# One load per projection weight, x brought in transposed, and a sample tile in column quarters, in a convolutional decoder layer on eight cores

## The chip, the cores and the metric

The kernel runs on the eight NeuronCores of one Trainium2 chip, two dies of four cores. Every core executes the same program on its own part of the batch, and no core waits for another. The metric is the device time in microseconds (us) of the slowest core of one execution, taken as the median of several executions. An execution counts as slow when one die is more than 1% longer than the other at a lower granted TensorE clock, or when it is more than 1.5% above the fastest execution of the same kernel; only fast executions are compared below. The granted clock is the share of its full clock that the profile's records show TensorE was given. TensorE writes its results into banks of a buffer called PSUM, which the other engines read and so free again. Loads are issued on two queues, GpSimd's and SyncE's, and both are served by the same 16 transfer (DMA) engines of the core. Engine names in the profile are PE (TensorE), PEld (weight load of TensorE), DVE (VectorE), ACT (ScalarE), POOL (GpSimd) and SP (SyncE, which here only issues transfers).

## The reference

One layer of a trunk, applied to 8 prompt sequences of 2048 tokens (one for each core) and to 128 single sample tokens (16 for each core). The width D is 1024, the hidden width of the two feed-forward networks (FFN) 2816.

```python
def swiglu(x, w_gate, w_up, w_down):
    return (silu(x @ w_gate) * (x @ w_up)) @ w_down

def token_mixers(h, ctx_a, ctx_b, w_in, b_in, w_dw_a, ...):
    z = h @ w_in + b_in                                    # 1024 -> 2560
    a_val, a_gate, g_b, g_c, b_val = split(z, 5 parts of 512)
    u = a_val * sigmoid(a_gate)
    ua, new_ctx_a = causal_depthwise(ctx_a, u, w_dw_a)     # width 31
    ua = silu(layer_norm(ua + b_dw_a, ln_conv_g, ln_conv_b))
    v = g_c * b_val
    vb, new_ctx_b = causal_depthwise(ctx_b, v, w_dw_b)     # width 3
    out = concatenate([ua, g_b * vb]) @ w_o + b_o
    return out, new_ctx_a, new_ctx_b

def trunk_layer(x, ...):
    x = layer_norm(ALPHA * x + 0.5 * swiglu(x, first FFN))
    x = layer_norm(ALPHA * x + token_mixers(x))
    x = layer_norm(ALPHA * x + 0.5 * swiglu(x, second FFN))
    return x, new_a, new_b
```

The outputs are the new x of the prompts and of the samples, and the last 30 and last 2 inputs of the two convolutions.

## The kernel before

A core treats its 2048 + 16 tokens in two blocks (1024 and 1040). `xT` holds x transposed, in bf16, for all tokens; `hT` holds the hidden activations of one block; `RW` is one large buffer that holds the down weights during a down-projection and the mixer's work space between. Every engine executes its list of instructions in the order in which the program emits them, and a small helper, `P.op`, puts a semaphore wait wherever one instruction reads or overwrites what another engine or a transfer has touched. It goes by names such as `("xr", s)`.

An up-projection is a list of groups. One group is 16 matmuls of up to 512 columns (8 for the gate, 8 for the up half), a SiLU pass on ScalarE and a multiplication on VectorE:

```python
def u_group(idx, b, f, g):
    (tok0, n, gi) = g
    l0 = tok0 - b * BLK
    s = idx % NSLOT
    bg, bu, q = ub(), ub(), sgr()

    def mm(e, gu, bk):
        for k in range(KC):
            c = (gu * KC + k) * 128
            ins = e.matmul(bank(bk, n), lhsT=ring[:, s, c:c + 128], rhs=xT[:, k, tok0:tok0 + n],
                           start=(k == 0), stop=(k == KC - 1))
        return ins
    P.op("pe", lambda e: mm(e, 0, bg), reads=[("ring", s, 0)] + xtoks(tok0, n), writes=pst(bg))
    P.op("pe", lambda e: mm(e, 1, bu), reads=[("ring", s, 1)] + xtoks(tok0, n), writes=pst(bu))
    P.op("act", lambda e: e.activation(out=sg[:, q, :n], in_=bank(bg, n), func=AF.Silu),
         reads=pst(bg), writes=[("sg", q)])
    P.op("dve", lambda e: e.tensor_tensor(out=hT[:, f, l0:l0 + n], in0=sg[:, q, :n], in1=bank(bu, n), op=ALU.mult),
         reads=[("sg", q)] + pst(bu), writes=[("hT", f, gi)])

```

`merge` lays other work between the groups. Each item of the second list has a gap: how many up groups follow it. So the mixer of a block is hidden among the matmuls of the next up-projection.

```python
def merge(items, side):
    credit = 0.0
    items = list(items)
    for th, gap in side:
        th()
        credit += gap
        while credit >= 1.0 - 1e-9 and items:
            items.pop(0)()
            credit -= 1.0
    while items:
        items.pop(0)()
```

x is loaded in rows and transposed on TensorE, as is every normed tile that a later matmul reads:

```python
def xpose_from(t, src, rtoks, bk):
    (tok0, n) = tok(t)

    def pe(e):
        for k in range(KC):
            ins = e.transpose(out=psb[:, bk * 1024 + k * n: bk * 1024 + (k + 1) * n],
                              in_=src[:n, k * 128:(k + 1) * 128], identity=ident_bf[:n, :n])
        return ins
    P.op("pe", pe, reads=list(rtoks) + ["ident_bf"], writes=pst(bk))
    P.op("act", lambda e: e.activation(
        out=xT[:, :, tok0:tok0 + n],
        in_=psb[:, bk * 1024: bk * 1024 + KC * n].rearrange("p (k n) -> p k n", k=KC), func=AF.Identity),
        reads=pst(bk), writes=[("xT", t)])
```

The mixer before goes unit by unit, a unit being 512 tokens: for each of four channel chunks five projections (each with its own load of the weight), the convolution input written to DRAM and read back in replicas that are shifted by one token, and 32 matmuls in four column groups. Then follow, per tile of 128 tokens, a norm, SiLU, the output projection (with the bias as a matmul of two rows) and the second norm.

```python
        win_seq = [fo for u in range(4) for ch in range(4) for fo in (4 + ch, ch, 12 + ch, 16 + ch, 8 + ch)]
# ... (in tA)
                P.op("sp", lambda e: e.dma_start(out=uscr[us], in_=U[:, us, :]),
                     reads=[("U", us), ("Uh", us), ("Uz", us)] + MC, writes=[("uscr", us)], dma="us_%d" % us)
# ... (in rep_in)
                for s_ in range(4):
                    P.op("sp", lambda e, s_=s_: e.dma_start(out=R2[32 * s_:32 * s_ + 32, :, :], in_=src[:, :, s_:s_ + R2W]),
                         reads=[("uscr", us)] + MC, writes=[("R2", s_)], dma="r2_%d" % s_)
# ... (in S3)
                    for k in (4, 5, 6, 7, 0, 1, 2, 3):
                        for h in range(2):
                            e.matmul(ps[:n, (4 + h) * 512:(5 + h) * 512], lhsT=lhs(k), rhs=wo[:, k, h * 512:(h + 1) * 512],
                                     start=(k == 4), stop=False)
                    for h in range(2):
                        ins = e.matmul(ps[:n, (4 + h) * 512:(5 + h) * 512], lhsT=ones2[0:2, :n],
                                       rhs=bo2[0:2, h * 512:(h + 1) * 512], start=False, stop=True)
```

The program at its top level, after the first loads. Transposes of x stand between the first up groups, and the lines with `merge` show what is laid beside what:

```python
        for t in range(2):
            x0pose(t)
        u_group(0, 0, 0, (0, 256, 0))
        for t in range(2, 4):
            x0pose(t)
        u_group(0, 0, 0, (256, 256, 0))
        u_group(1, 0, 1, (0, 512, 0))
# ...
        ss = sample_state()
        side = [(lambda: (consts(), ss[0](), load_ln(0)), 2)]
        for i in range(11):
            side.append((lambda i=i: load_wd(0, i), 1.0))
            side.append((ss[1 + i] if i < len(ss) - 1 else (lambda: None), 2.2))
        merge(up_items(0, 0)[4:], side)
# ...
        pend = down(0, 0, 2.0 * ALPHA, 4.0 * EPS, False, aux=aux)
# ...
        merge(up_items(0, 1), side)                     # side: mixer(0, ...)
        load_ln(0)
        pend = down(0, 1, 2.0 * ALPHA, 4.0 * EPS, False, npar=3)
# ...
        merge(up_items(1, 0), side)                     # side: mixer(1, ...)
        load_ln(2)
        down(1, 0, 2.0 * ALPHA, 4.0 * EPS, True, npar=3)
        merge(up_items(1, 1), [])
        down(1, 1, 2.0 * ALPHA, 4.0 * EPS, True)
```

## Time and profile before

Three executions took 1312.84 to 1314.68 us, median 1312.9. A further one was profiled. All cores ran undisturbed: spans of 1295.9 to 1312.2 us, mean granted clock 0.984 to 0.991.

The prediction shows the lines of the page and of the nine stretches. This table is the key to them: idle time of PE in each stretch is its length less the busy time in it.

| Stretch | What runs | PE idle | What PE waits for |
|---|---|---|---|
| (1) | first FFN, up of block 0 | 29.8 | x, its transposes, the convolution state |
| (2) | its down | 1.6 | |
| (3) | up of block 1, mixer of block 0 | 6.5 | replicas of the convolution input |
| (4) | its down | 7.6 | transposes after the norm |
| (5) | second FFN, up of block 0, mixer of block 1 | 13.5 | transposes, replicas, small outputs |
| (6) | its down | 0.6 | |
| (7) | up of block 1 | 2.1 | a product of VectorE |
| (8) | its down | 0 | |
| (9) | after the last matmul | 10.2 | end of the last norm and store |

How to read it: PE is busy for 95% of the time, so what is not taken out of its list must come from the 72 us in which it stands, and some 40% of those are in the first stretch.

### The profile page before, as it was taken

Reading aid. Unit: us, or ns where it says so; the run is one execution under the profiler, and the core shown is the slowest. Engines: PE = TensorE matmul, PEld = TensorE weight load, DVE = VectorE, ACT = ScalarE, POOL = GpSimd, SP = SyncE. Lnnn points to the kernel's source line nnn. Section 1 sums busy time; section 2 is a strip of 40 time slices with the busy share of each in tenths; the row PEclk is TensorE's granted clock in tenths of the full one; section 3 lists DMA queues with packets and bytes.
Section 4 is the critical chain, followed back from the end, with each engine's and each line's share of the span. In section 5 each row is a group of like instructions: output and inputs, shape, how many; then the busy total and the mean of one; then the engine's idle time right before and its main releaser. Section 6 shows DMA issues by size and latency. Waiting matters only on the chain.

```text
span 1312.2 us, 20168 instructions; the slowest of 8 cores (1295.9 to 1312.2 us)
## 1 busy us (share of the span) xinstructions
PE 1240.5 (95%) x7262; PEld 645.5 (49%) x7262; DVE 527.4 (40%) x856; ACT 273.9 (21%) x460; POOL 211.3 (16%) x361
## 2 busy tenths in 40 slices
PE   5599999999999999998989899999999999999996
PEld 4244444445555556553444344445444456666443
DVE  0222124544445544515544345543633632222454
ACT  2111112231123313301121123313420011111000
POOL 2011102211122112111111112102220110000011
PEclk9899999999999999999999999999999999999999
DMA  9686769448865686793237856546777344442122
GB/s 137 132 180 112 123 111 179 135 118 148 168 124 126 136 164 118 159 198 107 67 102 142 163 110 134 123 89 132 148 177 146 128 113 80 69 79 33 51 82 81
DMA packets 65172, 161.54 MB, mean 123 GB/s; under 512 B 6882, under 2 KB 17506, under 8 KB 65059
## 3 DMA queue, kind: packets, MB, share of 16 engines
q0 software_dynamic: 36832, 90.75, 42.8%
q1 hardware_dynamic: 28243, 69.51, 16.6%
q8 instruction: 60, 0.98, 0.3%
q14 instruction: 37, 0.30, 0.1%
...
## 4 chain that ended last, share of the span: by engine, by line
PE 87%; DMA 6%; DVE 2%; issue 2%; ACT 1%; POOL 1%; SPq 0%; POOLq 0%; DVEq 0%; ACTq 0%
PE ps L457 44%; PE ps L521 23%; PE ps L576 10%; PE ps L806 4%; PE ps L694 2%; DMA sb_RW<-wd 2%; PE ps L396 2%; DMA sb_RW<-uscr 1%; DMA sb_hT<-sca 1%; DMA uscr<-sb_RW 1%; DMA sb_ring<-wgu 1%; PE ps L809 1%; PE ps L783 1%; PE ps L758 1%; DVE sb_xr L427 1%
## 5 line engine op out<-in xcount | busy, mean ns | idle before, releaser
L457 PE MATMUL ps<-sb_xT,sb_ring 128*128 128x352 bf16 (+3 forms) x3568 | 639.3, 338 | 13.9 <-ACT sb_xT L400 7.0
L457 PEld LDWEIGHTS ps<-sb_xT,sb_ring 128*128 128x128 bf16 x3568 | 347.9, 99 | 284.8 <-issue 30.6
L521 PE MATMUL ps<-sb_RW,sb_hT 128*128 128x512 bf16 (+1 forms) x1496 | 327.4, 380 | 0.6 <-DMA sb_RW<-wd 0.6
L464 DVE TENSOR_TENSOR sb_hT<-sb_sg,ps 128x352 bf16<-128x352 f32 (+3 forms) x223 | 129.0, 579 | 456.9 <-PE ps L457 399.1
L521 PEld LDWEIGHTS ps<-sb_RW,sb_hT 128*128 128x128 bf16 (+1 forms) x1496 | 145.2, 98 | 175.7 <-issue 3.5
L462 ACT ACTIVATE sb_sg<-ps 128x352 f32<-128x352 f32 (+3 forms) x223 | 113.5, 510 | 497.0 <-PE ps L457 395.9
L576 PE MATMUL ps<-sb_xT,sb_wring 128*128 128x512 bf16 (+1 forms) x800 | 150.4, 340 | 2.0 <-DVE sb_hT L464 1.3
L408 DVE SCALAR_TENSOR_TENSOR sb_xr<-sb_xr,ps 128x1024 f32<-128x1024 f32 (+1 forms) x51 | 62.2, 1219 | 172.4 <-PE ps L521 154.1
L337 POOL DMA_DIRECT2D sb_ring<-wgu x90 | 49.9, 558 | 412.4 <-PE ps L457 373.9
L576 PEld LDWEIGHTS ps<-sb_xT,sb_wring 128*128 128x128 bf16 x800 | 68.5, 98 | 78.6 <-issue 5.5
L416 POOL TENSOR_SCALAR sb_mv<-sb_mv 128x1 f32<-128x1 f32 (+1 forms) x51 | 16.0, 314 | 383.5 <-DVE sb_mv L414 383.4
L427 DVE SCALAR_TENSOR_TENSOR sb_xr<-sb_xr,sb_mv,sb_lnb 128x1024 f32<-128x1024 f32 (+1 forms) x51 | 65.5, 1284 | 21.4 <-POOL sb_mv L418 18.4
L350 POOL DMA_DIRECT2D sb_wring<-win x80 | 43.4, 543 | 174.1 <-PE ps L576 152.0
L384 ACT ACTIVATE sb_xb<-sb_xr 128x1024 bf16<-128x1024 f32 (+1 forms) x34 | 36.0, 1058 | 164.2 <-DVE sb_xr L427 164.2
L412 DVE BATCH_NORM_STATS2 sb_stt<-sb_xr 128x6 f32<-128x512 f32 (+1 forms) x102 | 65.6, 684 | 5.3
L424 DVE SCALAR_TENSOR_TENSOR sb_xr<-sb_xr,sb_mv,sb_lnb 128x1024 f32<-128x1024 f32 (+1 forms) x51 | 66.0, 1294 | 4.1
L400 ACT ACTIVATE sb_xT<-ps 128x1024 bf16<-128x1024 bf16 (+1 forms) x51 | 48.7, 978 | 72.0 <-PE ps L396 71.8
L806 PE MATMUL ps<-sb_wo,sb_RW 128*128 128x512 bf16 x256 | 57.9, 379 | 0.0
L418 POOL TENSOR_TENSOR sb_mv<-sb_mv,sb_neghalf 128x1 f32<-128x1 f32 (+1 forms) x51 | 53.8, 1055 | 7.9 <-POOL sb_mv L416 0.9
L806 PEld LDWEIGHTS ps<-sb_wo,sb_RW 128*128 128x128 bf16 x256 | 24.9, 98 | 29.0 <-issue 0.4
L694 PE MATMUL ps<-sb_RW,sb_dgb 128*32 128x512 bf16 x512 | 31.8, 392 | 7.5 <-DMA sb_RW<-uscr 6.7
L396 PE MATMUL ps<-sb_ident_bf,sb_xb 128*128 128x128 bf16 (+1 forms) x272 | 20.7, 219 | 11.4 <-ACT sb_xb L384 11.4
...
## 6 DMA issues: line engine op xcount, KB each, us to landing
...
```

What stands on the lines that cost most here:

```text
L408: P.op("dve", lambda e: e.scalar_tensor_tensor(out=xr[:n, s, :], in0=xr[:n, s, :], scalar=in_scale, in1=ps[:n, bk * 512:(bk + 2) * 512], o ...
L412: P.op("dve", lambda e, h=h: e.bn_stats(out=stt[:n, m, h, :], in_=xr[:n, s, h * 512:(h + 1) * 512]), reads=[("xr", s)], writes=[("stt", m, ...
L418: P.op("pool", lambda e: e.tensor_tensor(out=mv[:n, m, 2:3], in0=mv[:n, m, 3:4], in1=neghalf[:n, 0:1], op=ALU.pow), reads=[("ve", m), "neg ...
L424: P.op("dve", lambda e: e.scalar_tensor_tensor(out=xr[:n, s, :], in0=xr[:n, s, :], scalar=mv[:n, m, 0:1], in1=lnb[:n, 0, :], op0=ALU.subtr ...
L427: P.op("dve", lambda e: e.scalar_tensor_tensor(out=xr[:n, s, :], in0=xr[:n, s, :], scalar=mv[:n, m, 2:3], in1=lnb[:n, 1, :], op0=ALU.mult, ...
L457: ins = e.matmul(bank(bk, n), lhsT=ring[:, s, c:c + 128], rhs=xT[:, k, tok0:tok0 + n], start=(k == 0), stop=(k == KC - 1))
L462: P.op("act", lambda e: e.activation(out=sg[:, q, :n], in_=bank(bg, n), func=AF.Silu), reads=pst(bg), writes=[("sg", q)])
L464: P.op("dve", lambda e: e.tensor_tensor(out=hT[:, f, l0:l0 + n], in0=sg[:, q, :n], in1=bank(bu, n), op=ALU.mult), reads=[("sg", q)] + pst( ...
L521: ins = e.matmul(ps[:n, (yb + h) * 512:(yb + h + 1) * 512], lhsT=hT[:, f, l0:l0 + n], rhs=wd[:, f, h * 512:(h + 1) * 512], start=(f == 0), ...
L576: ins = e.matmul(bank(bk, n), lhsT=wring[:, slot, k * 128:(k + 1) * 128], rhs=xT[:, k, tok0:tok0 + n], start=(k == 0), stop=(k == KC - 1))
L694: ins = e.matmul(ps[32 * g_:32 * g_ + 32, bk * 512:(bk + 1) * 512], lhsT=dgb[:, ds_, q * 128 + 32 * g_: q * 128 + 32 * g_ + 32], rhs=R2[:, ...
L806: e.matmul(ps[:n, (4 + h) * 512:(5 + h) * 512], lhsT=lhs(k), rhs=wo[:, k, h * 512:(h + 1) * 512], start=(k == 4), stop=False)
```

## The change

The intent has four parts. First, each weight of the input projection is loaded once per block of 1024 tokens instead of once per 512, and both halves of the block use it; the norm and output part then follows as a whole. Second, x and the sample's convolution state come in already transposed (the host lays them out), so the transposes go. Third, the 16 sample tokens no longer use TensorE's whole width of 512 columns with 16 columns of weights: the output is cut into four quarters of 256 columns, which go to four column groups side by side, and four small transfers gather them again. Fourth, the output bias moves from a matmul into a table that VectorE adds, and the last tile's norm is done in two halves. The core of the diff, cut:

```diff
+    xt = din("xt", [SEQ // XPC, 128, KC * XPC])          # XPC = 256
+    scat = din("scat", [128, 4 * NS * 30])
# ...
-        win_seq = [fo for u in range(4) for ch in range(4) for fo in (4 + ch, ch, 12 + ch, 16 + ch, 8 + ch)]
+        win_seq = [fo for b in range(2) for ch in range(4) for fo in (4 + ch, ch, 12 + ch, 16 + ch, 8 + ch)]
# ...
+        def quarter_gather(bk):
+            P.op("act", lambda e: e.activation(out=sgx[:, :], in_=bank(bk, 256), func=AF.Identity),
+                 reads=pst(bk), writes=[("dgb", 0)])
+            s2 = xrr()
+            for j in range(4):
+                P.op("sp", lambda e, j=j: e.dma_start(out=xr[:NS, s2, 256 * j:256 * j + 256], in_=sgx[32 * j:32 * j + NS, :]),
+                     reads=[("dgb", 0)], writes=[("xr", s2)], dma="xq%d_%d" % (s2, j))
+            return s2
# ... (in down)
+                def peq(e):
+                    for f in range(lo, hi):
+                        for j in range(4):
+                            ins = e.matmul(ps[32 * j:32 * j + NS, yb * 512:yb * 512 + 256], lhsT=hT[:, f, l0:l0 + NS],
+                                           rhs=wd[:, f, 256 * j:256 * j + 256], start=(f == 0), stop=(f == NFC - 1),
+                                           tile_position=(0, 32 * j))
+                    return ins
# ... (in S3: no bias matmuls)
-                       rhs=bo2[0:2, h * 512:(h + 1) * 512], start=False, stop=True)
+                            ins = e.matmul(ps[:n, (4 + h) * 512:(5 + h) * 512], lhsT=lhs(k),
+                                           rhs=wo[:, k, h * 512:(h + 1) * 512], start=(k == 4), stop=(k == 3))
# ... (sample_state)
-                for r in range(4):
-                    P.op("sp", ... in_=sca[r * 128: r * 128 + rows, :]), ...)
+                P.op("sp", lambda e: e.dma_start(out=CA, in_=scat.rearrange("p (c t) -> p c t", c=4)),
+                     writes=["CA"] + [k for r in range(4) for k in hrow(10 + r)], dma="sa")
# ...
+                P.op("sp", lambda e: e.dma_start(out=nas3[:, :, :], in_=sca3[:, 1:30, :]), dma="st_nas0")
# ... (start)
-        fetch_x0(0)
-        fetch_x0(1)
+        fetch_xt(0)
         fetch_wgu(0, 2)
-        fetch_x0(2)
-        fetch_x0(3)
+        fetch_xt(1)
         fetch_wgu(1, 2)
# ... (consts)
+            load_ln(0)
+            P.op("sp", lambda e: e.dma_start(out=lnp[:, :], in_=bod.to_broadcast([128, D])), writes=["lnp"], dma="c_bo")
+            P.op("dve", lambda e: e.scalar_tensor_tensor(out=lnp[:, :], in0=lnp[:, :], scalar=1.0 / ALPHA, in1=lnb[:, 1, :],
+                                                         op0=ALU.mult, op1=ALU.add),
+                 reads=["lnp", ("lnb", 1)], writes=["lnp"])
# ...
+        ev = [(3, ss[0]), (6, consts), (12, ss[1])] + [(4.5 + 3.8 * i, lambda i=i: load_wd(0, i)) for i in range(9)]
# ...
         merge(up_items(0, 0)[4:], side)
+        for i in range(9, 11):
+            load_wd(0, i)
# ...
-        pend = down(0, 1, 2.0 * ALPHA, 4.0 * EPS, False, npar=3)
+        pend = down(0, 1, 2.0 * ALPHA, 4.0 * EPS, False, npar=2)
# ...
-        side = [(lambda: None, 1.0), (lambda p=pend: xpose(*p, mb()), 0.5)] + mixer(1, 1, 0.5, 0.6, 1.0)
-        merge(up_items(1, 0), side)
+        merge(up_items(1, 0), mixer(1, 1, pend, 2.0, 0.65, 0.7))
```

Here `ss[0]` is the list of state loads and copies and `consts` the list of tables; the first number of each pair in `ev` is the up group after which it stands.

## The prediction

> **What bounds the kernel now.** I read the page first (busy times), then PE alone in nine stretches cut at the changes of stage, then the groups by shape, then who waits for whom, and last PE's order of time around each long wait.
>
> ```profile
> PE 1240.5 (95%) x7262; PEld 645.5 (49%) x7262; DVE 527.4 (40%) x856; ACT 273.9 (21%) x460; POOL 211.3 (16%) x361
> ```
>
> TensorE is the bound; nothing else passes 49%. A change helps by giving PE fewer or shorter instructions, or by closing the 5% in which PE stands. The stretches (start:end, length, PE busy, granted clock, DMA share, GB/s) show where PE stands:
>
> ```profile
> core 5: us, PE busy (x), PEclk, DMA share, GB/s
> 0.00:195.75 195.75, 165.97 (x837) 0.96 0.75 133
> 195.75:280.49 84.74, 83.17 (x481) 1.00 0.63 137
> 280.49:572.48 291.99, 285.53 (x1912) 1.00 0.75 149
> 572.48:671.29 98.81, 91.20 (x462) 0.98 0.40 100
> 671.29:980.37 309.08, 295.62 (x1770) 0.99 0.66 134
> 980.37:1057.09 76.72, 76.13 (x353) 1.00 0.54 135
> 1057.09:1216.35 159.26, 157.18 (x1058) 0.99 0.40 74
> 1216.35:1302.02 85.67, 85.67 (x396) 1.00 0.22 76
> 1302.02:1312.20 10.18, 0.00 (x0) 0.72 0.13 52
> ```
>
> In order: (1) first up-projection of block 0, (2) its down, (3) up of block 1 with the mixer of block 0 beside it, (4) its down, (5) second FFN's up of block 0 with mixer 1, (6) its down, (7) up of block 1, (8) its down, (9) the tail after PE's last matmul. Idle PE: 29.8 us in (1), 7.6 in (4), 13.5 in (5), 6.5 in (3); the others are nearly full. Groups by shape that the change touches (count | busy, mean ns | idle before):
>
> ```profile
> L694 PE MATMUL ps<-sb_RW,sb_dgb 128*32 128x512 bf16 x512 | 31.8, 392 | 7.5 <-DMA sb_RW<-uscr 6.7 <-DVE sb_RW L636 0.8
> L521 PE MATMUL ps<-sb_RW,sb_hT 128*16 128x512 bf16 x88 | 19.3, 379 | 0.0
> L809 PE MATMUL ps<-sb_bo,sb_ones 2*128 2x512 bf16 x32 | 9.6, 379 | 0.0
> L396 PE MATMUL ps<-sb_ident_bf,sb_hT 128*128 128x128 bf16 x64 | 6.0, 264 | 9.3 <-DMA sb_hT<-xp 9.3
> L396 PE MATMUL ps<-sb_ident_bf,sb_wring 128*128 128x128 bf16 x64 | 4.9, 219 | 0.0
> ```
>
> Means of single matmuls overlap; busy over count is the cost. The sample tile (16 tokens) pays a full 219 ns per matmul in both downs. The waits of PE:
>
> ```profile
> PE ps L893 <- DMA sb_hT<-sca: 12.9, 1, 12.9
> PE ps L396 <- ACT sb_xb L384: 11.4, 5, 5.1
> PE ps L396 <- DMA sb_hT<-xp: 9.3, 2, 8.3
> PE ps L457 <- ACT sb_xT L400: 7.0, 5, 1.8
> PE ps L694 <- DMA sb_RW<-uscr: 6.7, 2, 5.1
> ```
>
> Each concerns something the change takes out or moves: the transpose of the convolution state, the transpose after a norm, the load and transpose of x, the replicas of the convolution input.
>
> **What the Trainium skill says.** "TensorE: Matmul & The Clock Gate", Part 1: after an idle window of about 3.4 us the PE clock falls to half until PE has been busy for such a window. The trace agrees: after the 12.9 us wait the granted clock is 0.50 from 53.8 to 67.5 us, after the 5.1 us waits in (4) and (5) it is 0.50 for 3.4 us. So a long wait costs its length and about 1.7 us more. The same page, "Back-to-back issue gap": N/2.4 + 2.5 ns warm, 215.8 at N = 512; the trace has 9.50 us for 44, 215.9. "TensorEngine Tiling (Array Packing)", Key Properties: column tiles run matmuls in parallel. The trace shows it in the convolution (L694): 32 matmuls of 512 columns in four column groups took 1.84 us, 57.5 ns each. "DMA: Bandwidth & Descriptors", Queues, rings and completion order: each DMA engine goes round-robin between the queues that have work. The trace has the DMA share near 1 from 3 to 30 us with GpSimd's queue alone, so a second queue there must take from the first.
>
> **The change part by part.** The order of instructions shows equal counts for the main work: 3568 up, 1408 full down, 640 + 160 projection, 512 convolution, 256 output matmuls. "One load of each weight" halves the transfers of projection weights (80 to 40, 256 KB each as written), not PE's work. These transfers land in 5.5 us and PE never waits for them, so this alone buys nothing.
>
> Taken from PE:
> - x transposes: 128 of 128 columns + 8 small. In (2) eight groups of eight take 0.44 us, the sample's group with its waits about 2: 5.7 us. The 64 in (1) belong to the start, below.
> - Output bias: 32 + 2 matmuls, (9.6 + 0.6) us busy less overlap, 34 x 266 ns start to start = 9.0; 4.2 in (3), 4.8 in (5). It comes back as one VectorE pass for each of 17 first-FFN tiles (1.29 us, which replaces ScalarE's cast of 1.06), in the 9.5 us that PE needs for a tile: hidden.
> - Sample tile in column quarters: 44 matmuls of 512 become 88 of 256 in four groups. At 512 columns such a matmul cost 57.5; halved is 29, but 16-column matmuls cost 42.6 ns start to start here, so I take 40: 88 x 40 = 3.5 us for 9.6, saving 6.1 in (4) and 6.1 in (8). In the output projection 16 x 219 becomes 32 x 40: 2.2 in (5). The gathering DMAs get a whole tile of time.
> - Transposes of the state (20) and of the small outputs (16): 16 to 20 at 0.11 us, 2 us in (1), 1.9 in (5).
>
> Moved, by stage:
> - (1) The start. At 61.9 us PE has done 24.0 us of up-projection (13.65 for two f chunks, then three groups at 3.45); the rest takes until 195.75. After: no transposes, no wait for the state. But SyncE's queue formerly stopped at the bias round trip (40 us); now nothing holds back its state, table, norm and x loads, 5.3 MB. By packet durations 1 MB takes 3.1 us of all 16 engines on SyncE's queue and 6.2 (as written in bf16) on GpSimd's: 17 + 4.2 x 6.2 = 26, or 43 us of a full DMA system from 3 us on. The first eight loads, landed by 34 before, land by about 46; x and first weights at about 20 instead of 15. I walk PE through them: chunks 0 and 1 done at 44.5, chunks 2 and 3 at 58.3 (2 x 6.9). That is 27.3 us of work; 124.8 remain, plus 3 for a VectorE burst and clock loss: ends at 186. Saves 10, not 24.
> - (2) 84.7 - 5.7 = 79, but the last two down weights are now queued on GpSimd behind the 22nd chunk's prefetch, which waits for the end of (1). Three such loads land at about 6, 8.5 and 11 us; tile 0 wants the last at 8.6. Plus 2.5: 81.5.
> - (3) Busy 285.5 - 4.2 + 0.4 (one transpose group more) = 281.7; idle about 3 instead of 6.5, as convolution inputs now have some 25 us; new short waits where the norm part starts alone. 284.5.
> - (4) Transposes follow one tile later and only two tiles are interleaved, so the 5.1 and 1.2 waits go with the half clock: 91.2 - 6.1 - 1.7 - 0.4 + 1.5 idle = 84.5.
> - (5) 295.6 - 4.8 - 2.2 - 1.9 + 0.4 - 3 (half clocks after 2.4 and 5.1 us waits) + 5 idle = 289.
> - (6) 76.7. (7) 159.3 less 2 from a fourth PSUM bank for the up groups (the 2.08 wait at 1061.7 and its half clock): 157.
> - (8) 85.7 - 6.1 = 79.6. (9) The last tile's norm in halves: the adding pass and statistics of half one lie under the matmuls and each half is stored when ready: 10.2 - 1.5 = 8.7.
>
> Sum: 186 + 81.5 + 284.5 + 84.5 + 289 + 76.7 + 157 + 79.6 + 8.7 = 1247.5; 1248 us, 5% less.
>
> **The rivals.** (a) The start eats its gain: SyncE's loads delay x and weights so much that the half clock returns; (1) ends at 196 as before, total 1258, or 1270 with two more stalls. For: DMA share near 1 until 30 us. Against: before, DMA was almost idle from 33 to 39, so there is slack to use. (b) Column quarters do not run side by side for 16-wide weights (each waits for its predecessor): 88 x 107 ns = 9.4, nothing saved in (4), (5), (8): plus 13, total 1261. Against: L694. (c) The norm part of the mixer, now without projections beside it, becomes a chain of short waits: transposes wait for VectorE, GpSimd, ScalarE (0.7 + 0.2 + 0.15 + 0.6 + 0.3 + 0.8 us plus semaphores, over 3 us) with one up group of 2.4 between the first steps. 16 tiles at 0.7: plus 11, total 1259. Against: later steps have two to four groups. VectorE, at 65 of 95 us there, stays below PE. (d) Waits were all that held PE back and all go: 1235.
>
> **Range and chances.** PE-only removals (some 26 us outside the start) are nearly certain; waits removed are likely, the start is the loosest term. One rival leaves 1258 to 1261, two near 1271; rival (d) 1235. Range 1232 to 1270. Two per cent is 1286.6: it would take three rivals together or a new stall of 25 us. Chances: faster 0.95, same 0.045, slower 0.005.
>
> **What would show it.** Right: PE's first matmul near 20 us, (1) ending near 186; no wait for state or x; sample matmuls near 40 ns each; no wait of the convolution on its replicas; busy PE near 1205; a wait of 2 to 3 us for the down weights in tile 0 of (2). Wrong: a long PE wait on DMA or a clock of 0.50 between 20 and 45 us; VectorE releasing the up groups for many microseconds in the norm part; a sample tile near 9 us.

## The result, and the profile after

The changed kernel is correct and takes 1280.1 us (median of four executions), against 1313.09 for the kernel before in the same rounds. Its fast executions took 1280.91, 1279.29 and 1278.43 (median 1279.3, with which the runs below are compared); the fourth, 1437.45, was slow, with one die at a granted clock of 0.86 and the other at 0.99. The ratio of the fast runs is 0.9742, with a 95% interval of 0.9723 to 0.9761. Ratios here are the mean time of one kernel's fast runs over that of the other's fast runs of the same rounds, so they are not quite the ratio of the medians that are quoted beside them. The direction of the prediction was right, but 1280 lies outside its range of 1232 to 1270.

The busy times on the page of the kernel after, which answer to the first line shown of before:

```profile
PE 1198.1 (94%) x7160; PEld 626.7 (49%) x7160; DVE 537.7 (42%) x884; ACT 235.7 (18%) x420; POOL 198.4 (16%) x315
```

PE's own work fell by 42 us, from 1240.5 to 1198.1, while the time fell by only 33. So PE stands longer than before: 81.2 us instead of 71.7. The same nine stretches, PE alone (start:end, length, PE busy, granted clock, DMA share, GB/s):

```profile
core 3: us, PE busy (x), PEclk, DMA share, GB/s
0.00:191.51 191.51, 156.66 (x753) 1.00 0.87 133
191.51:279.39 87.88, 80.71 (x402) 0.96 0.65 126
279.39:574.88 295.49, 282.08 (x1907) 0.99 0.66 132
574.88:656.54 81.66, 81.66 (x498) 1.00 0.49 125
656.54:952.76 296.22, 285.10 (x1763) 0.99 0.61 126
952.76:1032.76 80.00, 77.83 (x354) 0.98 0.44 124
1032.76:1189.37 156.61, 155.33 (x1058) 1.00 0.40 75
1189.37:1268.12 78.75, 78.75 (x442) 1.00 0.24 83
1268.12:1279.36 11.24, 0.00 (x1) 0.71 0.13 48
```

The reader should compare busy with length in each row. Rows (4) and (8) are full, and row (7) has 1.3 us of idle time left. Rows (1), (2), (3), (5) and (6) have 34.9, 7.2, 13.4, 11.1 and 2.2 us of idle time. Set beside the prediction:

| Stretch | Before | Predicted | After | After less predicted |
|---|---|---|---|---|
| (1) | 195.75 | 186 | 191.51 | +5.5 |
| (2) | 84.74 | 81.5 | 87.88 | +6.4 |
| (3) | 291.99 | 284.5 | 295.49 | +11.0 |
| (4) | 98.81 | 84.5 | 81.66 | -2.8 |
| (5) | 309.08 | 289 | 296.22 | +7.2 |
| (6) | 76.72 | 76.7 | 80.00 | +3.3 |
| (7) | 159.26 | 157 | 156.61 | -0.4 |
| (8) | 85.67 | 79.6 | 78.75 | -0.9 |
| (9) | 10.18 | 8.7 | 11.24 | +2.5 |
| Sum | 1312.2 | 1247.5 | 1279.4 | +31.8 |

The groups by shape (partitions x elements, count | busy, mean ns | idle before): the convolution, and the sample tile in both down-projections.

```profile
L762 PE MATMUL ps<-sb_RW,sb_dgb 128*32 128x512 bf16 x512 | 30.6, 380 | 0.0
L585 PE MATMUL ps<-sb_RW,sb_hT 128*16 128x256 bf16 x176 | 5.2, 273 | 0.0
```

The convolution no longer waits for its replicas (0.0 at the end of the line, 7.5 before). The sample's 176 small matmuls cost 5.2 us together where 88 large ones cost 19.3. The waits of PE:

```profile
PE ps L515 <- DMA sb_ring<-wgu: 31.8, 2, 31.2
PE ps L875 <- ACT sb_wring L865: 12.3, 4, 8.1
PE ps L579 <- DMA sb_RW<-wd: 9.3, 3, 3.7
PE ps L515 <- ACT sb_sg L520: 5.7, 4, 1.8
PE ps L515 <- DVE sb_hT L522: 4.4, 2, 3.2
```

In each line the first number is the sum, the second the count and the third the longest wait. Of the five waits shown of before only that for a cast of ScalarE is left, at 0.5 us; these five are new or larger. The largest is the first up group, which starts only at 31.22 us because its x landed at 25.62 and its first weights at 30.97.

The clock of 1.00 in row (1) hides something. The first clock record of this core is that of 1.00 at 43.9 us, and before it there is none. Until then matmuls of 256 columns start 213 ns apart, and from 46 us on 109 ns apart. So PE ran at half pace from 31.2 to 43.9 us, which the row does not show. The kernel before and runs 5 and 11 below begin at the same 213 ns.

Three places in the order of time carry the argument. First, PE at the beginning of the first down-projection (start, duration, line, tiles, count, wait in brackets):

```profile
191.51 7.93 PE L579 MATMUL ps<-sb_RW,sb_hT 128*128 128x512 bf16 x36
203.14 1.02 PE L579 MATMUL ps<-sb_RW,sb_hT 128*128 128x512 bf16 x4 [3.70 <-DMA sb_RW<-wd]
207.63 21.76 PE L579 MATMUL ps<-sb_RW,sb_hT 128*128 128x512 bf16 x92 [3.47 <-DMA sb_RW<-wd]
```

PE stops twice for the last down weights, and the granted clock is 0.50 from 204.4 to 211.2 us. Second, the sample's gather in (5), from several engines (SPq is SyncE's queue):

```profile
890.94 10.63 SPq L418 DMA_DIRECT2D sb_xr<-sb_dgb  x3
902.93 1.21 DVE L426 SCALAR_TENSOR_TENSOR sb_xr<-sb_xr 16x1024 f32<-16x1024 f32 x1 [10.75 <-DMA sb_xr<-sb_dgb]
910.43 1.09 PE L875 MATMUL ps<-sb_ident,sb_wring 128*128 128x128 f32 x4 [8.05 <-ACT sb_wring L865]
```

Three of the four small transfers are issued over 10.63 us, VectorE stands 10.75 us before its first pass on the gathered row, and PE then stands 8.05. Third, the norm part of the first mixer, in (3):

```profile
506.10 0.27 POOL L862 TENSOR_SCALAR sb_mvc<-sb_mvc 128x1 f32<-128x1 f32 x1 [0.18 <-POOL sb_mvc L860]
506.46 0.78 ACT L865 ACTIVATE sb_wring<-ps,sb_mvc 128x512 f32<-128x512 f32 x1 [2.73 <-POOL sb_mvc L862]
507.14 0.45 ACT L520 ACTIVATE sb_sg<-ps 128x352 f32<-128x352 f32 x1
507.74 1.30 PE L515 MATMUL ps<-sb_xT,sb_ring 128*128 128x336 bf16 x8 [1.20 <-ACT sb_sg L520]
```

ScalarE stands 2.73 us at a pass of the norm (L865) whose mean comes from GpSimd; behind it in its list is the SiLU pass of an up group (L520), which could have run at once. PE waits 1.20 us for that SiLU.

### The profile page after: what moved, and what is told of

Read it like the earlier page. It is cut to its first block, busy times and chain, and to the rows that moved or that the text cites. A ratio compares the mean times of both kernels' runs of the same rounds, so it can differ in the third digit from the quotient of the medians.

```text
span 1279.4 us, 19773 instructions; the slowest of 8 cores (1271.3 to 1279.4 us)
## 1 busy us (share of the span) xinstructions
PE 1198.1 (94%) x7160; PEld 626.7 (49%) x7160; DVE 537.7 (42%) x884; ACT 235.7 (18%) x420; POOL 198.4 (16%) x315
## 4 chain that ended last, share of the span: by engine, by line
PE 83%; DMA 7%; DVE 4%; issue 3%; POOL 2%; ACT 1%; DVEq 0%; POOLq 0%; ACTq 0%; SPq 0%
PE ps L515 43%; PE ps L579 22%; PE ps L658 11%; PE ps L906 4%; DMA sb_xT<-xt 3%; DMA sb_RW<-wd 2%; PE ps L762 2%; DMA sb_xr<-sb_dgb 1%; PE ps L404 1%; DMA sb_wring<-win 1%; DVE sb_xr L426 1%; DVE sb_stt L430 1%; PE ps L875 1%; DVE sb_sttc L855 0%; POOL sb_mvc L860 0%
## 5 line engine op out<-in xcount | busy, mean ns | idle before, releaser
L515 PE MATMUL ps<-sb_xT,sb_ring 128*128 128x352 bf16 (+3 forms) x3568 | 637.9, 337 | 45.3 <-DMA sb_ring<-wgu 31.8
L515 PEld LDWEIGHTS ps<-sb_xT,sb_ring 128*128 128x128 bf16 x3568 | 347.6, 98 | 316.2 <-issue 56.8
L579 PE MATMUL ps<-sb_RW,sb_hT 128*128 128x512 bf16 x1408 | 310.3, 382 | 9.3 <-DMA sb_RW<-wd 9.3
L579 PEld LDWEIGHTS ps<-sb_RW,sb_hT 128*128 128x128 bf16 x1408 | 137.9, 98 | 176.1 <-issue 15.5
L520 ACT ACTIVATE sb_sg<-ps 128x352 f32<-128x352 f32 (+3 forms) x223 | 113.5, 509 | 531.0 <-PE ps L515 418.4
L434 POOL TENSOR_SCALAR sb_mv<-sb_mv 128x1 f32<-128x1 f32 (+1 forms) x50 | 47.0, 939 | 393.1 <-DVE sb_mv L432 393.1
L426 DVE SCALAR_TENSOR_TENSOR sb_xr<-sb_xr,ps 128x1024 f32<-128x1024 f32 x47 | 57.2, 1218 | 113.5 <-PE ps L579 105.8
L445 DVE SCALAR_TENSOR_TENSOR sb_xr<-sb_xr,sb_mv,sb_lnb 128x1024 f32<-128x1024 f32 (+1 forms) x33 | 42.4, 1284 | 18.7 <-POOL sb_mv L436 15.8
L442 DVE SCALAR_TENSOR_TENSOR sb_xr<-sb_xr,sb_mv,sb_lnb 128x1024 f32<-128x1024 f32 (+1 forms) x33 | 42.3, 1281 | 1.7
L358 POOL DMA_DIRECT2D sb_wring<-win x40 | 21.6, 541 | 117.2 <-PE ps L658 116.5
L906 PE MATMUL ps<-sb_wo,sb_RW 128*128 128x512 bf16 x128 | 30.2, 379 | 1.6 <-DVE sb_xr L426 1.6
L436 POOL TENSOR_TENSOR sb_mv<-sb_mv,sb_neghalf 128x1 f32<-128x1 f32 (+1 forms) x50 | 30.4, 607 | 7.7 <-POOL sb_mv L434 0.4
L906 PE MATMUL ps<-sb_wo,sb_wring 128*128 128x512 bf16 x128 | 30.2, 379 | 0.0
L455 DVE SCALAR_TENSOR_TENSOR sb_xb<-sb_xr,sb_mv,sb_lnb 128x1024 bf16<-128x1024 f32 (+1 forms) x17 | 21.8, 1284 | 16.2 <-POOL sb_mv L436 15.2
```

The source lines that it names most:

```text
L426: P.op("dve", lambda e: e.scalar_tensor_tensor(out=xr[:n, s, :], in0=xr[:n, s, :], scalar=in_scale, in1=add, op0=ALU.mult, op1=ALU.add), r ...
L434: P.op("pool", lambda e: e.tensor_scalar(out=mv[:n, m, 3:4], in0=mv[:n, m, 1:2], scalar1=eps, scalar2=None, op0=ALU.add), reads=[("mv", m) ...
L445: P.op("dve", lambda e: e.scalar_tensor_tensor(out=xr[:n, s, :], in0=xr[:n, s, :], scalar=mv[:n, m, 2:3], in1=lnb[:n, 1, :], op0=ALU.mult, ...
L579: ins = e.matmul(ps[:n, (yb + h) * 512:(yb + h + 1) * 512], lhsT=hT[:, f, l0:l0 + n], rhs=wd[:, f, h * 512:(h + 1) * 512], start=(f == 0), ...
L906: ins = e.matmul(ps[:n, (4 + h) * 512:(5 + h) * 512], lhsT=lhs(k), rhs=wo[:, k, h * 512:(h + 1) * 512], start=(k == 4), stop=(k == 3))
```

## The experiments

The first theory after this reading: the gain went into waits that the change itself made, (a) SyncE's state and table loads that stand ahead of x in the transfer engines, (b) the last two down weights, which are issued too late, (c) the four gather transfers, each of which waits for the landing of the one before, since all four write the same name `("xr", s2)`. The rival: the transfers as such fill the machine (DMA share 0.87 in (1)), and whatever is moved, something else will wait. Eleven kernels ran, all correct, each beside the kernel before on one chip (1310.8 to 1318.1 us, 21 executions, all fast). Runs 1 to 4, 5 to 8 and 9 to 11 were on three different chips; the ratios allow for that. The table gives all fast times; slow executions are counted and left out.

| Run | Fast runs, us | Slow runs | Ratio to before, 95% |
|---|---|---|---|
| 1 SyncE's loads wait | 1275.86, 1275.37, 1279.20 | 1 | 0.9724 (0.9699 to 0.9750) |
| 2 down weights early | 1273.61, 1275.89, 1272.96 | 1 | 0.9704 (0.9680 to 0.9728) |
| 3 gather at once | 1269.33, 1268.68, 1272.85 | 2 | 0.9665 (0.9637 to 0.9692) |
| 4 all three | 1255.15, 1257.73, 1256.78 | 3 | 0.9570 (0.9547 to 0.9593) |
| 5 tables late too | 1242.53, 1241.68, 1243.06, 1241.53 | 0 | 0.9456 (0.9433 to 0.9479) |
| 6 weights twice | 1244.37, 1246.39, 1246.57 | 1 | 0.9489 (0.9454 to 0.9523) |
| 7 sample full width | 1258.71, 1257.10, 1257.06, 1256.80 | 0 | 0.9572 (0.9549 to 0.9595) |
| 8 other spacing | 1236.42, 1234.28, 1236.19, 1236.02 | 1 | 0.9407 (0.9384 to 0.9430) |
| 9 x in blocks of 512 | 1280.39, 1282.52, 1282.50, 1281.21 | 0 | 0.9750 (0.9733 to 0.9767) |
| 10 state copy moved | 1276.01, 1274.43, 1278.44, 1276.89 | 0 | 0.9711 (0.9688 to 0.9734) |
| 11 best | 1228.53, 1230.53, 1228.69, 1228.80 | 0 | 0.9350 (0.9334 to 0.9366) |

And the lengths of the stretches that differ, from the profile of the slowest core of each. Runs 1, 2, 4, 9 and 10 change the kernel after; 5 builds on 4; 6, 7 and 8 on 5; 11 on 8. The profile of run 3 fell into a slow execution, so its stretches are not used.

| Stretch | After | 1 | 2 | 4 | 5 | 6 | 7 | 8 | 9 | 10 | 11 |
|---|---|---|---|---|---|---|---|---|---|---|---|
| (1) | 191.5 | 187.8 | 191.5 | 184.8 | 171.4 | 172.3 | 170.8 | 170.8 | 194.2 | 185.1 | 170.6 |
| (2) | 87.9 | 87.3 | 78.7 | 78.7 | 78.7 | 78.7 | 78.7 | 78.7 | 87.8 | 87.4 | 78.7 |
| (3) | 295.5 | 296.6 | 295.7 | 297.2 | 296.0 | 302.7 | 297.2 | 294.8 | 294.1 | 296.8 | 291.3 |
| (4) | 81.7 | 81.7 | 81.7 | 81.7 | 81.7 | 81.7 | 88.7 | 81.7 | 81.7 | 81.7 | 81.7 |
| (5) | 296.2 | 296.8 | 297.5 | 286.8 | 286.0 | 286.6 | 288.2 | 284.0 | 296.5 | 297.1 | 284.0 |
| (8) | 78.8 | 78.8 | 78.8 | 78.8 | 78.8 | 78.5 | 85.6 | 78.8 | 78.8 | 78.8 | 78.8 |
| (9) | 11.2 | 11.2 | 11.2 | 11.2 | 11.2 | 9.5 | 11.2 | 9.5 | 11.2 | 11.2 | 7.4 |

### Run 1: SyncE's loads wait for the fourth block of x

The first of SyncE's loads gets a dependence on the block of x that lands last among the first four; the others stand behind it in SyncE's list.

```diff
-                P.op("sp", lambda e: e.dma_start(out=CA, in_=scat.rearrange("p (c t) -> p c t", c=4)),
+                P.op("sp", lambda e: e.dma_start(out=CA, in_=scat.rearrange("p (c t) -> p c t", c=4)), reads=xtoks(768, 256),
                      writes=["CA"] + [k for r in range(4) for k in hrow(10 + r)], dma="sa")
```

> The changed kernel, with SyncE's first loads (state, tables, norm vectors, x tiles) waiting until the fourth x block of 256 tokens has landed. My theory: the DMA engines serve GpSimd's and SyncE's queue one packet each in turn, so x's 512-byte packets lost against packets of up to 59392 bytes; without the competitor the first x block lands near 9 us instead of 25.6, the first matmul starts near 13.5 instead of 31.2, and the first up-projection ends near 173 instead of 191.5; total near 1261. Rival: x's 512-byte packets are slow by themselves; then the first block still lands after 18 us and the total falls by less than 6 us.

Measured: the first block of x landed at 9.8 us instead of 25.62 and PE's first matmul came at 13.31 instead of 31.22, as expected. But (1) ended at 187.8, only 3.7 us earlier, and the total came down some 3 us (1275.9 against 1279.3, with ratio intervals that overlap) instead of the 19 expected. The order of time of run 1 shows why:

```profile
75.50 1.22 DVE L1055 SCALAR_TENSOR_TENSOR sb_lnp<-sb_lnp,sb_lnb 128x1024 f32<-128x1024 f32 x1 [16.72 <-DMA sb_lnp<-bo]
77.47 4.73 PE L515 MATMUL ps<-sb_xT,sb_ring 128*128 128x512 bf16 x14 [15.23 <-DVE sb_hT L522]
```

VectorE reached the pass that builds the bias table (L1055) 16.72 us before the bias had landed, at 75.33. It executes in order, so the products of the up groups behind it stood, PSUM was not freed, and PE stood 15.23 us; the granted clock was half from 67.0 to 80.7. What follows: the start is delayed by SyncE's loads, as theory (a) says, and the expectation overlooked one consumer of them. The rival has the total's number (less than 6 us), but not its cause: the block landed at 9.8, and in run 1 x's packets of 512 bytes take 66 ns each, 8.1 us of all 16 engines for 1 MB, the same for each byte as the packets of 2048 bytes beside them (264 ns). So small packets cost no more here; they only get a smaller share beside large ones.

### Run 2: all down weights in the first up-projection

```diff
-        ev = [(3, ss[0]), (6, consts), (12, ss[1])] + [(4.5 + 3.8 * i, lambda i=i: load_wd(0, i)) for i in range(9)]
+        ev = [(3, ss[0]), (6, consts), (12, ss[1])] + [(4.5 + 3.2 * i, lambda i=i: load_wd(0, i)) for i in range(11)]
# ...
-        for i in range(9, 11):
-            load_wd(0, i)
```

> The changed kernel, with all eleven down-weight loads of the first FFN issued during the up-projection (as before the change), none after it. Theory: the two waits of 3.7 and 3.5 us in tile 0 of the first down, with the half clock after them, come only from the queue position of the last two loads; the first down falls from 87.9 to about 79, total near 1271. Rival: DMA is the bound there and the wait moves to another load (the up-weights or the x blocks of the second half): total within 3 us of the changed kernel.

Measured: (2) took 78.7 us instead of 87.9, as expected, with (1) unchanged at 191.5. The total came down by about 6 us (1273.6 against 1279.3), not the full 9: the slowest core of the kernel after had the longest (2) of the eight, the median core 86.5. Theory (b) holds, and nothing else began to wait.

### Run 3: the four gather transfers in one go

They are issued as one operation on one semaphore, and VectorE waits for all four.

```diff
-            for j in range(4):
-                P.op("sp", lambda e, j=j: e.dma_start(out=xr[:NS, s2, 256 * j:256 * j + 256], in_=sgx[32 * j:32 * j + NS, :]),
-                     reads=[("dgb", 0)], writes=[("xr", s2)], dma="xq%d_%d" % (s2, j))
+            def four(e):
+                for j in range(4):
+                    ins = e.dma_start(out=xr[:NS, s2, 256 * j:256 * j + 256], in_=sgx[32 * j:32 * j + NS, :])
+                    if j < 3:
+                        ins.then_inc(P.sem("xq%d" % s2), 16)
+                return ins
+            P.dma_cnt["xq%d" % s2] = P.dma_cnt.get("xq%d" % s2, 0) + 48
+            P.op("sp", four, reads=[("dgb", 0)], writes=[("xr", s2)], dma="xq%d" % s2)
```

> The changed kernel, with the four transfers that gather the sample's column quarters issued together on one semaphore instead of each waiting for the one before (they share one dependence token). Theory: the four chained transfers took 18.6 us in the second mixer and held VectorE and then PE for 8.0 us, and for half clock after it; together they take some 6 us: the stretch of up-projection and second mixer falls from 296 to about 285, total near 1269. Rival: the sample tile at the head of the norm part is late for other reasons (norm chain, DMA load) and PE still waits over 4 us there; total falls by less than 4 us.

Measured: 1269.33, 1268.68 and 1272.85 us in fast runs, as expected. In the kernel after, the four were issued at 884.22, 890.94, 897.37 and 901.06 and landed at 890.87, 897.30, 900.99 and 902.83: each issue follows the landing before it. In run 5, which keeps this edit, they were issued from 855.56 to 857.56 and landed from 860.92 to 863.20, 7.6 us in all instead of 18.6. Theory (c) holds.

### Run 4: the three edits together

> The three edits together. If the three causes are separate and sit in separate stages, the gains add: 1280 less 19, 9 and 11, near 1241 and inside 1235 to 1250. If the DMA work only moves from one stage to the next, the sum is much less: over 1255.

Measured: 1256.8 us, not 1241. (2) and (5) are at 78.7 and 286.8, so two of the three gains add up; (1) ended at 184.8 because the wait for the bias table of run 1 is still there. That wait makes 12 of the 16 us of the miss (184.8 where 173 was expected). The total alone lies where the rival put it, over 1255; it is the stretches that speak against it, as none but these three moved by more than 2 us.

### Run 5: the table passes later

The loads stay where they are; VectorE's two passes on them move from the 6th to the 24th up group.

```diff
+
+        def tables():
             P.op("dve", lambda e: e.tensor_scalar(out=hbg[:, :], in0=cst[:, C_BIN + 4:C_BIN + 8], scalar1=0.5, scalar2=None,
# ...
-        ev = [(3, ss[0]), (6, consts), (12, ss[1])] + [(4.5 + 3.2 * i, lambda i=i: load_wd(0, i)) for i in range(11)]
+        ev = [(3, ss[0]), (6, consts), (12, ss[1]), (24, tables)] + [(4.5 + 3.2 * i, lambda i=i: load_wd(0, i)) for i in range(11)]
```

> The three edits of the run before, and the two VectorE passes that build tables from SyncE's loads (half gate bias, norm bias plus output bias) placed 18 up groups later. Theory: in the run with SyncE's loads held back the first matmul did come at 13.3 us, but VectorE then stood in its own order before the table pass until the output bias landed at 75.3 us, and PE waited 15.2 us for it, with half clock after. With the passes late, the first up-projection ends near 173 instead of 185, total near 1244. Rival: DMA is simply too full in the first 80 us and the up weights become the wait; the stretch stays above 181.

Measured: 1242.1 us (mean of four fast runs 1242.2), as expected. The first stretch of run 5, in the form used above:

```profile
0.00:171.44 171.44, 154.53 (x752) 1.00 0.94 155
```

Twenty us went from (1) with nearly the same busy time (154.5 against 156.7), and the DMA share rose from 0.87 to 0.94. This settles it between the theory and its rival: the transfers were not the limit of the stretch, even with two more down weights in it; their order was. Runs 1 and 5 together show that one fault covered the other: to delay the loads alone only moved most of the wait to VectorE's table pass, and it went when the pass was moved as well.

### Run 6: each projection weight fetched twice

The headline of the change is one load of each weight. To see what it is worth, run 6 adds to run 5 a second transfer of each weight, to an unused place in DRAM. It is not the old kernel's second load to the same buffer, but as many transfers of the same size.

```diff
+                def two(e):
+                    e.dma_start(out=wdum[s, :, :], in_=win[win_seq[i]]).then_inc(P.sem("wring%d" % s), 16)
+                    return e.dma_start(out=wring[:, s, :], in_=win[win_seq[i]])
+                P.dma_cnt["wring%d" % s] = P.dma_cnt.get("wring%d" % s, 0) + 16
+                P.op("pool", two, writes=[("wring", s)], dma="wring%d" % s)
```

> The version with tables late, but each projection weight is fetched twice, the second copy to a scratch area in memory that nobody reads: as many transfers as before the change. Theory: the projection weights are hidden behind PE work, so one load instead of two is worth nothing: total within 3 us of the version with tables late. Rival: the halved traffic is part of the gain: 6 us or more slower, in the two mixer stretches.

Measured: 1246.4 us, 4 more than run 5, with ratio intervals that overlap. PE now waits for projection weights:

```profile
PE ps L667 <- DMA sb_wring<-win: 5.5, 3, 3.0
```

In run 5 these waits come to 1.2 us. The slowest core's (3) is 302.7, but the median of the cores is 297.2 against 295.4. The tail of run 6 is 1.7 us shorter than that of run 5 for a reason that has nothing to do with the loads (see (9) below), so the stretches before it lost some 6. The result lies between what the two theories expected and is not conclusive; it puts the single load's worth at a few us, out of the 33 of the change and the 71 of the change mended.

### Run 7: the sample tile at full width again

Run 5 with the column quarters and their gather taken out.

```diff
-                if t == 16:
-                    P.op("pe", peq, reads=rd, writes=pst(yb))
-                elif h_outer:
+                if h_outer:
# ...
-                if t == 16:
-                    late = (i, quarter_gather(pairs[i]))
-                    pre(i + nsk)
-                    continue
# ... (and in S3)
-                P.op("pe", peq if t == 16 else pe, reads=rt + [("wo", q) for q in range(4)] + WR + ["RM7"], writes=pst(4, 2))
+                P.op("pe", pe, reads=rt + [("wo", q) for q in range(4)] + WR + ["RM7"], writes=pst(4, 2))
```

> The version with tables late, but the sample tile is computed in two halves of 512 columns as before the change, without the gather. Theory: quarters run side by side (28.5 ns a matmul in the trace of the changed kernel), so undoing them costs 7 us in each of the two downs of block 1 and 2.5 in the second mixer: total 15 to 18 us slower. Rival: the shorter matmuls only uncover other waits and the gather costs as much: under 5 us slower.

Measured: 1257.1 us, 15 more than run 5, as expected: (4) took 88.7 instead of 81.7, (8) 85.6 instead of 78.8 and (5) 288.2 instead of 286.0. So the column quarters are worth 15 us where the gather is done at once; in the kernel after some 10 us of that (run 3: 1269.3 against 1279.3) are lost again in the chained gather.

### Run 8: another spacing of the mixer among the up groups

A new theory for (3): after the mended parts it still has 13 us of idle time, because the norm part stands too close, with one up group for each step. So the projections are packed closer and the norm part wider; the rival is that the order within ScalarE's list makes the waits, which spacing does not change.

```diff
-        merge(up_items(0, 1), mixer(0, 0, pend, 3.0, 1.0, 1.0))
+        merge(up_items(0, 1), mixer(0, 0, pend, 3.0, 0.8, 1.35))
# ...
-        merge(up_items(1, 0), mixer(1, 1, pend, 2.0, 0.65, 0.7))
+        merge(up_items(1, 0), mixer(1, 1, pend, 2.0, 0.55, 0.82))
```

> The version with tables late, with the up groups dealt out differently among the mixer's steps: 0.8 instead of 1.0 after each projection step and 1.35 instead of 1.0 after each norm step in the first mixer, 0.55 and 0.82 instead of 0.65 and 0.7 in the second. Theory: the new idle time of the first mixer (13.4 us where 3 were expected) is the norm part's chain of short waits with too little PE work between its steps: the stretch falls from 295 to about 288, total 6 to 8 us faster. Rival: the waits only move to the projection part, or come from the order of work on ScalarE and VectorE whatever the spacing: within 2 us.

Measured: 1236.1 us, 6 less than run 5, which is what the total was expected to lose, but not where it was expected: (3) went from 296.0 to 294.8 only, where 288 was expected; (5) lost 2.0 and the tail 1.7, and the tail's part has another cause, a closing instruction of GpSimd (see (9) below). The waits for SiLU stood where they were:

```profile
PE ps L520 <- ACT sb_sg L525: 5.7, 4, 2.2
```

(L520 and L525 are here what L515 and L520 are in the kernel after, where the sum is 5.7 too.) So the theory of spacing falls for (3), and the match of the total is no support for it.

### Run 9: x in blocks of 512 tokens

The kernel after with larger blocks of x, to test why x lands late. If the transfer engines share their time between two queues by packets, a block of 512 tokens, which has as many packets as one of 256 but each twice as large, lands hardly later; if by bytes or time, much later.

```diff
-XPC = 256
+XPC = 512
# ...
-        fetch_xt(1)
         fetch_wgu(1, 2)
-        fetch_xt(2)
-        fetch_xt(3)
+        fetch_xt(1)
```

> The changed kernel with x coming in in blocks of 512 tokens instead of 256: the same number of packets in a block (1024), each twice as long (1 KB as written). Theory: the engines give each queue one packet in turn whatever its length, so a block of 512 lands about when one of 256 did (25.6 us): between 24 and 29 us, and tokens 256 to 511 come 10 us or more earlier; first matmul stays near 31 us; first up-projection ends 3 to 5 us earlier, total near 1276. Rival: the queues share by bytes or time; then the double block lands after 33 us and the first matmul after 36 us.

Measured: the first block landed at 28.3 us, against 25.62 for half the tokens. That is in the range expected on the profiled cores and speaks for packets rather than bytes; over all eight cores it is 28.3 to 30.7 against 24.0 to 27.1, so most are a little beyond the 29 expected and none near the rival's 33. PE began at 33.29, between the 31 and the 36 of the two theories. The total did not gain (1281.9, and (1) took 194.2, where 3 to 5 us less were expected): the second block is whole only at 47.2, and PE stood 4.2 us for it. So twice the data in as many packets landed some 3 to 4 us later, and larger blocks of x gained no time.

### Run 10: the copy of the state moved

SyncE's list starts with a copy of most of the old convolution state to the output, memory to memory. In the kernel after alone, this copy and its small companion move to the first down-projection.

```diff
-                P.op("sp", lambda e: e.dma_start(out=nas3[:, :, :], in_=sca3[:, 1:30, :]), dma="st_nas0")
-                P.op("sp", lambda e: e.dma_start(out=nbs, in_=scb3[:, 1, :]), dma="st_nbs0")
# ...
+        def copies():
+            P.op("sp", lambda e: e.dma_start(out=nas3[:, :, :], in_=sca3[:, 1:30, :]), reads=xtoks(768, 256), dma="st_nas0")
+            P.op("sp", lambda e: e.dma_start(out=nbs, in_=scb3[:, 1, :]), dma="st_nbs0")
# ...
+        aux[3].append(copies)
```

> The changed kernel with the copy of the old convolution state from memory to memory (16 packets of 59392 bytes and 16 of 2048) moved from the start into the first down-projection. Theory: such a packet holds its engine for some 7 us in which the other queue gets nothing; without it the first x block lands near 17 us instead of 25.6 and the first matmul near 22 instead of 31. As the DMA system stays full, only the 7 us or so of copying leave the start: the first up-projection ends 4 to 7 us earlier, total near 1275. Rival: the copy shares like everything else, 0.95 MB of 5.3: first block at 23 us or later, total within 2 us.

Measured: x landed at 21.05 and PE began at 26.0, 4 us later than expected; (1) took 185.1, 6.4 us less, as expected; the total was 1276.5, near the 1275 expected, but that is only 3 us less than the kernel after, with ratio intervals that overlap. The large packets took 3.3 to 5.4 us each in the kernel after, not some 7. So the copy makes some 5 us of the delay of the first matmul; run 1, which holds back all of SyncE's loads, puts the whole at 17.9 (31.22 to 13.31), and the other loads are the rest. Both are read from (1), not from the total.

### Run 11: the best version

Run 8 with two more edits. ScalarE's pass of the norm is emitted one step later, behind the SiLU passes that can run at once. And SyncE at the end waits only for the transfers that nothing has waited for yet.

```diff
+        held = []
+        def free_held():
+            while held:
+                held.pop(0)()
# ... (S1)
-                P.op("act", lambda e: e.activation(out=xnc[:n, sl, :], in_=pv, func=AF.Identity,
-                                                   scale=mvc[:n, m, 2:3], bias=mvc[:n, m, 3:4]),
-                     reads=pst(bk) + [("rsc", m), ("nmc", m)] + WR, writes=[("xnc", sl)])
+                held.append(lambda: P.op("act", lambda e: e.activation(
+                    out=xnc[:n, sl, :], in_=pv, func=AF.Identity, scale=mvc[:n, m, 2:3], bias=mvc[:n, m, 3:4]),
+                    reads=pst(bk) + [("rsc", m), ("nmc", m)] + WR, writes=[("xnc", sl)]))
# ...
-                side.append((th, gE))
+                side.append((lambda th=th: (free_held(), th()), gE))
# ... (finalize)
-        final = [(self.sems[s], v) for s, v in self.dma_cnt.items()]
+        final = [(self.sems[s], v) for s, v in self.dma_cnt.items() if waited.get(s, 0) < v]
```

> The paced version, with ScalarE's pass that writes the normed convolution output queued one norm step later (after the SiLU of the up group in between), and the final waits left only on the seven transfers that no instruction has waited for. Theory: PE's 5.7 us of waits for the SiLU in the first mixer come from ScalarE standing at that pass, in its own order, for GpSimd; they fall below 2 us, waits for the pass itself grow by at most 2: the stretch of mixer one falls by 3 to 4 us. SyncE walks its 78 final waits at 50 ns each, past the last landing; with seven the tail loses 1.5 us. Total near 1231. Rival: the wait is on GpSimd and VectorE whatever ScalarE's order, then PE waits as long for the pass as it did for the SiLU: total within 2 us of the paced version's 1236.

Measured: 1228.7 us, ratio 0.9350, as expected: 6.5% less than the kernel before and 4% less than the kernel after. (3) took 291.3 instead of 294.8 (median of the cores 290.9 instead of 293.4), the tail 7.4 instead of 9.5, with 7 final waits instead of 72 (run 8 has 72; the 78 of the expectation are those of the kernel after). The waits for SiLU and the page's busy times in run 11 (L525 and L530 are the lines L515 and L520 of the kernel after):

```profile
PE ps L525 <- ACT sb_sg L530: 2.0, 1, 2.0
```

```profile
PE 1192.1 (97%) x7160; PEld 626.2 (51%) x7160; DVE 538.6 (44%) x884; ACT 238.3 (19%) x420; POOL 202.9 (17%) x315
```

The waits fell from 5.7 to 2.0, so the order in ScalarE's list was the cause of most of them. PE's busy share is 97% where it was 94%.

Of 52 executions of the changed kernel and the experiments ten were slow; none of the 25 of the kernel before was. In these one die, in one case both, ran at granted clocks of 0.81 to 0.96 and the time was 1300 to 1478 us. Runs 5, 7, 9, 10 and 11 had none in four executions each, so the counts do not tie it to an edit. Why it comes, and whether the change makes it more frequent, stays open.

## Why the prediction was right or wrong

The mechanism was right: TensorE bounds, and instructions taken from it come off the time. The range was missed because the waits in the sum were too small: in (1), (2), (3), (5) and (6) by 33.4 us together, and the tail (9) by 2.5, against 4.1 us that (4), (7) and (8) did better.

**The counts of PE's work held.** Busy PE was predicted near 1205 and is 1198. In (3) it was predicted at 281.7 and is 282.1.

**The sample tile in quarters was worth more.** The prediction took 40 ns for each small matmul. The 176 of both down-projections took 5.0 us from start to start, 28.5 ns each, so 2.5 us for each down instead of the 3.5 predicted. The 40 came from 42.6 ns start to start for matmuls of 16 columns, but that mean includes the groups of 16 after which PE stood (1.2 to 1.4 us up to the next matmul); an undisturbed group of 16 took 0.41 us, 25.5 ns each. One us for each down is what (8) gained over the prediction (0.9), and with the 1.5 us of idle time allowed in (4), which did not come, it makes up most of (4)'s 2.8. Rival (b), that the quarters do not run side by side, fell, and run 7 confirms the size.

**(1), "x and first weights at about 20 instead of 15": x came at 25.6 and the weights at 31.0.** This is the step that failed in the start. The first eight loads, which the prediction has landed by about 46, were there at 54.5, and PE stood for 3.1 us more before 38.58. Rival (a), that SyncE's loads delay x and the weights, came true, though (1) ended at 191.5 and not at its 196. The wording of the step shares the engines' time between the two queues. The trace shows that the queues share by count of packets. These are the packets that started in windows of 3 us, counted from the per-packet records of the kernel after:

| us | GpSimd's queue (x, weights) | SyncE's queue |
|---|---|---|
| 15 to 18 | 286, all of 512 B | 290, of up to 4096 B |
| 18 to 21 | 201, nearly all of 512 B | 203, mostly 4096 B |
| 21 to 24 | 139 | 131, mostly 4096 B |
| 24 to 27 | 77 | 82, mostly 4096 B |
| 27 to 30 | 123 | 122, mostly 4096 B |
| 30 to 33 | 401 | 180, mostly 4096 B |
| 33 to 36 | 671 | 31 |

From 15 to 30 us, while both queues have work, the counts are equal within 7%, though x comes in pieces of 512 bytes and the tables in pieces of 4096. From 18 to 21 us GpSimd's queue had 0.81 us of the engines' 3.04 us of packet time, and moved 102 KB where SyncE's moved 737. From 31 us on SyncE's loads run out, and from 33 the first queue starts 671 packets in 3 us. Before 12 us the copy of the state adds its part with pieces of 59392 bytes: between 9 and 12 us both queues together started 22 packets, which agrees with run 10. The Trainium skill's page "DMA: Bandwidth & Descriptors", Queues, rings and completion order, which the prediction cites, says that the engines go round-robin at the level of packets; I had used the rule but weighed it by time instead. The change itself made this worse: in the kernel before x came in packets of 2048 bytes, in the kernel after in packets of 512. One reading of the prediction was also wrong: from 3 to 9 us of the kernel before GpSimd's queue was not alone, SyncE's started 252 packets there. The prediction's "DMA was almost idle from 33 to 39, so there is slack to use" was true, but the slack lies after the moment at which x is wanted.

The same term had a second error in the other direction. "Saves 10, not 24" was the choice between two numbers; run 5 shows that 24 was to be had (195.75 to 171.4), with edits that only move loads and two short VectorE passes.

**(2), "Plus 2.5": it was 7.2 of waits and the half clock.** The two late weights landed at 203.0 and 207.39, that is 11.5 and 15.9 us after the stretch began, where the prediction had the last load at about 11; from issue to landing they took 10.3 and 14.0 us. The mechanism was named in the prediction, and run 2 confirms it; the transfer times were taken as too short. Why they were so long was not tested; the DMA share of the stretch is 0.65.

**(3), "idle about 3 instead of 6.5": it was 13.4.** The prediction's rival (c) named this chain of short waits and gave it 11 us, for both mixers together, then set it aside with "later steps have two to four groups". Waits of this kind cost PE 9.3 us in (3), 5.7 for the SiLU and 3.6 for ScalarE's norm pass; that the excess of (3), 11.0, equals the rival's figure is luck, for 3.2 us of the idle time have another cause. The waits for SiLU (5.7) come from ScalarE's order; run 11 shows it. Others are 3.2 at the start of the stretch, where three norm passes of VectorE are still to be done, and 3.6 where the norm part begins. For these two I have the order of time but no experiment, and in run 11, at 291.3, they (3.2 and 2.9) and 7 us above the predicted 284.5 are still there. That part stays open.

**(5), "The gathering DMAs get a whole tile of time": they needed more.** The step failed not in the length of one transfer, 1.8 to 6.7 us there, but in that the program chains the four: they share one name, so each waits for the one before, 18.6 us in all. That is visible in the code, and the prediction did not look. VectorE's wait of 10.75, PE's of 8.05 and 6.8 us of half clock follow. Runs 3 and 4 show it: (5) falls to 286.8, below the predicted 289.

**(6)** had 2.2 us of waits for down weights on core 3 and a half clock from 968.9 to 972.4. Across the runs it took 76.0 to 80.7; the prediction's 76.7 is at the lower end of that. The median core of the kernel after took 77.1, so most of the 3.3 belongs to the slowest core alone.

**(9), "10.2 - 1.5 = 8.7": it was 11.2.** The last of the half stores landed at 1276.13, 8.0 us after PE's end. Then SyncE walks through its final waits, 78 of them where the kernel before has 65, some 50 ns each, until 1277.64. But what ends last is GpSimd's closing DRAIN, the instruction by which it finishes its list: it ran from 1270.41 to 1279.13. The first line is from the kernel after, the second from the kernel before:

```profile
L166 POOLq DRAIN  x1: 8719/8719/8719, 1270.4 to 1270.4; - x1
L165 POOLq DRAIN  x1: 4951/4951/4951, 1305.6 to 1305.6; - x1
```

It took 8.7 us on every core of the kernel after and of runs 1 to 5, 7, 9 and 10, and 4.9 to 5.1 us in the kernel before and in runs 6, 8 and 11, where it ends before SyncE's waits or with them. This is why the tail is 9.5 in runs 6 and 8; with seven final waits as well it is 7.4 in run 11. The prediction looked at the norm and the stores alone, and why the DRAIN is long in some programs stays open.

**(7)** held: 157 predicted, 156.6 measured, and the wait at the beginning of the stretch is shorter, 1.28 us instead of 2.08, with no half clock after it. The fourth PSUM bank did not remove it, and no run takes the bank back. The statement that one load of each weight "alone buys nothing" is not settled: run 6 lost 4 us, some 6 without its shorter tail, with intervals that overlap, and its second copies went to memory.

## What to carry to other kernels

A load that nobody needs soon was not free at the start of this kernel: while both queues had work, each got as many packets as the other, and the one with small packets lost; make late loads depend on the early ones, and then move the in-order passes that consume the late loads as well. Several transfers that fill parts of one buffer should not share one dependence name, or they run one after the other. When PE is at 95%, work out the waits that a change makes as carefully as the instructions that it removes: here PE's busy time was right within 1%, and between the kernel after and run 11 waits alone, with the half clock that follows them and the shorter tail, were worth 51 us, more than the 42 us of work that the change took out.

## What the Trainium skill lacked or had wrong

- "DMA: Bandwidth & Descriptors", Queues, rings and completion order: round-robin at packet level agrees with this trace (286 against 290 packets, 201 against 203, 139 against 131), but the page does not draw the consequence that a queue of small packets gets a small share: 102 KB against 737 KB in 3 us with packets of 512 and 4096 bytes. What is counted here are the packet records of the profile; the page has several descriptors in a packet, and that the two are the same is not shown. In run 9 a block of x with packets twice as large landed 2.7 us later for twice the data on the profiled cores.
- "TensorE: Matmul & The Clock Gate", Part 1, warns that a die goes to 13/16 of the clock once three of its cores run dense matmuls, and stays there. Here eight cores at 94 to 97% busy PE had mean granted clocks of 0.98 to 1.00 in all fast executions; the ten slow ones of 52 had medians of a die from 0.81 to 0.96. So it is not to be budgeted as the rule for this kernel, and what decides between the two states for the same kernel I found on no page.
- The same page's half clock after a window of idleness agrees: 0.50 for 6.8 us after the gather's wait of 8.05 us, and for 3.4 us after shorter ones. The same page's "Back-to-back issue gap", which the prediction uses, gives its formula for an isolated matmul and some 131 ns for a stream at 512 columns; this trace has the formula's 215.9 ns in a stream of 44.
- No page that I read has the length of GpSimd's closing DRAIN: 8.7 us in nine of the kernels here and 4.9 to 5.1 us in the other four, all of it in the tail after PE's last matmul.
